# Storing the first five pairs of output batches two batches sooner in a batched matmul of two transposed operands

## The chip, the cores and the metric

The kernel runs on one core of a Trainium2 chip. The metric is the device time of one execution in microseconds (us), the median of several runs. The span that a profile shows is about 2 us shorter than the time measured for the same run. SyncE, ScalarE, VectorE and TensorE are called by these names; in the profile's lines they are SP, ACT, DVE and PE. A transfer between DRAM and SBUF, the core's working memory, is issued by SyncE or ScalarE, each of which has its own queue, and moved in packets by the core's 16 DMA engines. In the rows of 40 slices, DMA is the busy share of these engines in tenths (9 is 90% or more) and PEclk the clock granted to TensorE in tenths (9 is 90% or more, 5 is half).

## The reference

Sixteen independent products of 512 x 512 matrices, both operands transposed, in float32:

```python
def setup_inputs():
    batch, m, k, n = 16, 512, 512, 512
    return {"a": np.random.randn(batch, k, m).astype(np.float32),
            "b": np.random.randn(batch, n, k).astype(np.float32)}

def reference(a, b):
    return np.matmul(a.transpose(0, 2, 1), b.transpose(0, 2, 1)).astype(np.float32)
```

That is 33.55 MB to read and 16.78 MB to write.

## The kernel before

Batches go in eight pairs. SyncE's queue holds all loads, in program order, and at its end the stores of the last three pairs. ScalarE's queue holds the stores of pairs 0 to 4, between its casts and copies. VectorE casts and turns b (through TensorE's transposes); ScalarE casts a. There are three buffers for pairs of a, three for b, and five for pairs of output; the reuse of an output buffer is guarded by SyncE, which waits for an old store to land before it issues the load of a later pair's a.

```python
WIDE = range(1, 6)
LOADS = 3
PAIRS = 3
OUTS = 5
LAG = 3
TAIL = 3
H = B // 2
# ... cut ...
def run_sp(sp):
    for i in range(B):
        if i == 0:
            load_a(sp, 0)
        for p in ([0] if i == 0 else [(i + 1) // 2] if i % 2 and i + 1 < B else []):
            if p >= PAIRS:
                sp.wait_ge(turned, p - PAIRS + 1)
            sp.dma_start(b_sb[p % PAIRS][:], b_v[p]).then_inc(b_in[p % PAIRS], 16)
        if i % 2 == 0 and i // 2 >= OUTS:
            sp.wait_ge(o_out[i // 2 % OUTS], 16 * (i // 2 // OUTS))
        if i and not (i % 2 and i // 2 in WIDE):
            load_a(sp, i)
    for j in range(H - TAIL, H - 1):
        sp.wait_ge(summed, MO * (2 * j + 2) + 3)
        store(sp, j)
    # ... the last pair goes in two halves: cut ...

def run_act(act):
    cast_a(act, 0)
    for i in range(B - 1):
        cast_a(act, i + 1)
        copy_out(act, i, slice(2, 4), oa_go)
        j, odd = divmod(i - LAG, 2)
        if odd and 0 <= j < H - TAIL:
            store(act, j)
    # ... cut ...

# TensorE, per pair:
with pe.Fori(0, H) as _i:
    half(0, 0)
    half(0, 1)
    take(bt_go)
    turn(0)
    half(1, 0)
    turn(1)
    half(1, 1)
```

`cast_a(act, i)` waits for batch i's load; `half(x, h)` is half of a batch's sums, 8 matmuls. The loads of pairs 1 to 5 (WIDE) are one transfer of 2.1 MB in contiguous runs of 16 KB; batches 12 to 15 are loaded one by one, in runs of 8 KB, as stores are.

## Time and profile before

| | before |
|---|---|
| time, median | 124.49 us (124.38 to 124.84, 3 runs) |
| span of the profile | 122.5 us |
| bytes moved | 50.33 MB, of it 39.85 on SyncE's queue |
| TensorE, VectorE, ScalarE busy | 68%, 46%, 55% |
| a pair's loads at the full rate | 9.8 us |
| a pair's compute (stores of ScalarE at 43.55, 54.10, 64.66) | 10.5 us |

No engine is near its limit on the average; what is full is the transfers.

### The profile page before, as it was taken

Reading aid. Unit: us, or ns where it says so; the run is one execution under the profiler, and the core shown is the slowest. Engines: PE = TensorE matmul, PEld = TensorE weight load, DVE = VectorE, ACT = ScalarE, POOL = GpSimd, SP = SyncE. Lnnn points to the kernel's source line nnn. Section 1 sums busy time; section 2 is a strip of 40 time slices with the busy share of each in tenths; the row PEclk is TensorE's granted clock in tenths of the full one; section 3 lists DMA queues with packets and bytes.
Section 4 is the critical chain, followed back from the end, with each engine's and each line's share of the span. In section 5 each row is a group of like instructions: output and inputs, shape, how many; then the busy total and the mean of one; then the engine's idle time right before and its main releaser. Section 6 shows DMA issues by size and latency. Waiting matters only on the chain. (4 is left out here: it accounts for less than half of the span.)

```text
span 122.5 us, 1093 instructions
## 1 busy us (share of the span) xinstructions
PE 83.3 (68%) x400; PEld 48.0 (39%) x400; DVE 56.0 (46%) x48; ACT 66.9 (55%) x44; POOL 0.7 (1%) x6
## 2 busy tenths in 40 slices
PE   0000949799799979979994950593999599798000
PEld 0000913464365446437543610131744464374000
DVE  0005272837839575692759340039295542703000
ACT  4140015684997999799797008997221864803000
POOL 2000000000000000000000000000000000000000
PEclk9999999999999999999999997569999999999855
DMA  3999999999999999999999999999999999999992
GB/s 67 447 428 428 415 442 428 434 428 428 428 428 428 428 428 415 407 423 431 442 407 452 420 431 436 431 409 452 423 409 428 428 428 425 428 428 428 428 425 120
DMA packets 4928, 50.33 MB, mean 411 GB/s; under 512 B 448, under 2 KB 448, under 8 KB 448
## 3 DMA queue, kind: packets, MB, share of 16 engines
q1 hardware_dynamic: 3568, 39.85, 77.1%
q10 hardware_dynamic: 1360, 10.49, 20.2%
HBM read 33.55 MB, written 16.78 MB: 411 GB/s over the span
## 5 line engine op out<-in xcount | busy, mean ns | idle before, releaser
L256 PE MATMUL o_ps<-bt_sb,a_bf 128*128 128x512 bf16 x256 | 64.9, 402 | 8.7 <-PEq L231 8.2
L256 PEld LDWEIGHTS o_ps<-bt_sb,a_bf 128*128 128x128 bf16 x256 | 28.8, 116 | 38.7 <-issue 16.4
L164 ACT CAST a_bf<-a_sb 64x2048 bf16<-64x2048 f32 x20 | 38.0, 1899 | 7.6 <-DMA a_sb<-in_a_dram 7.3
L242 PE MATMUL bt_ps<-identity,b_bf 128*128 128x128 f32 x144 | 22.1, 302 | 20.8 <-PEq L231 20.8
L176 DVE COPY o_sb<-o_ps 128x1024 f32<-128x1024 f32 x16 | 19.6, 1224 | 29.9 <-PE o_ps L256 29.9
L242 PEld LDWEIGHTS bt_ps<-identity,b_bf 128*128 128x128 f32 x144 | 20.5, 209 | 25.7 <-issue 24.5
L189 DVE CAST b_bf<-b_sb 128x2048 bf16<-128x2048 f32 x16 | 19.4, 1219 | 22.7 <-DMA b_sb<-in_b_dram 22.7
L176 ACT COPY o_sb<-o_ps 128x1024 f32<-128x1024 f32 (+1 forms) x17 | 16.4, 964 | 19.7 <-PE o_ps L256 19.6
L166 ACT CAST a_bf<-a_sb 128x2048 bf16<-128x2048 f32 x6 | 11.4, 1901 | 18.4 <-DMA a_sb<-in_a_dram 18.4
L198 DVE COPY bt_sb<-bt_ps 128x1024 f32<-128x1024 f32 x16 | 19.4, 1214 | 2.7 <-PE bt_ps L242 2.7
L166 ACT ACT_TABLE_LOAD x1 | 1.3, 1283 | 0.9 <-PEq L302 0.9
L143 POOL TENSOR_SCALAR_AFFINE_SELECT identity<-identity 128x128 f32<-128x128 f32 x1 | 0.3, 292 | 0.2 <-POOL identity L141 0.2
L141 POOL MEMSET identity<- 128x128 f32 x1 | 0.2, 204 | 0.7 <-POOLq L54 0.7
L302 POOL MEMSET const-bfloat16-1.0<- 128x1 bf16 x1 | 0.1, 102 | 0.0
L302 POOL MEMSET const-uint8-127<- 128x1 uint8 x1 | 0.1, 102 | 0.0
L302 POOL MEMSET const-float32-0.0<- 128x1 f32 x1 | 0.1, 99 | 0.2 <-issue 0.2
L302 POOL MEMSET const-float32-1.0<- 128x1 f32 x1 | 0.1, 99 | 0.0
## 6 DMA issues: line engine op xcount, KB each, us to landing
b_sb<-in_b_dram SPq DMA_DIRECT2D x8, 2048.0 KB, 20.4
a_sb<-in_a_dram SPq DMA_DIRECT2D x5, 2048.0 KB, 19.0
out_dram<-o_sb ACTq DMA_DIRECT2D x5, 2048.0 KB, 16.2
a_sb<-in_a_dram SPq DMA_DIRECT2D x6, 1024.0 KB, 16.2
out_dram<-o_sb SPq DMA_DIRECT2D x2, 2048.0 KB, 13.3
out_dram<-o_sb SPq DMA_DIRECT2D x2, 1024.0 KB, 8.9
```

The costliest lines, as they stand in the source:

```text
L141: pool.memset(identity[:], 0.0).then_inc(id_go, 1)
L143: pool.affine_select(out=identity[:], in_=identity[:], compare_op=mybir.AluOpType.not_equal, fill=1.0, base=0, pattern=[[-1, P]], channel_ ...
L164: copy = act.copy(to[s * P // 2:(s + 1) * P // 2], x[own, s * KO:(s + 1) * KO, :])
L166: copy = act.copy(to[:], x[:, g * KO:(g + 1) * KO, :])
L176: copy(o_sb[i // 2 % OUTS][:, i % 2, rm, :], o_ps[h][:, p, :]).then_inc(go, 1)
L189: dve.tensor_copy(to, x).then_inc(bc_go, n)
L198: dve.tensor_copy(bt_sb[g][:].rearrange("p j (ni r) -> p j ni r", r=NR), bt_ps[:].rearrange("p j r (g ni) -> p g j ni r", g=2)[:, g],).the ...
L242: last = pe.transpose(bt_ps[:, j, r, :], w[:, r, j, :], identity[:])
L256: last = pe.matmul(o_ps[h][:, q, :], a_r[:, rk, 2 * h + q, :], bt_h[:, rk // 2, rk % 2, :], start=(rk == 0), stop=(rk == KO - 1),)
L302: nc = _bacc.Bacc("TRN2", target_bir_lowering=False, num_devices=1)
```

## The change

The intent: a pair is complete in SBUF when the batch behind it has been copied out, so it may be stored then. The output buffer comes free sooner, SyncE's waits for stores shrink, and the stores are spread over more of the run. Five stores on ScalarE's queue are each issued two batches sooner; nothing else moves.

```diff
-    LAG = 3
+    LAG = 1
```

## The prediction

> **What bounds the kernel now.** I read the page's slices first. The DMA row says 9 in every slice but the first and the last.
>
> ```profile
> span 122.5 us, 1093 instructions
> ...
> PE   0000949799799979979994950593999599798000
> ...
> DMA  3999999999999999999999999999999999999992
> GB/s 67 447 428 428 415 442 428 434 428 428 428 428 428 428 428 415 407 423 431 442 407 452 420 431 436 431 409 452 423 409 428 428 428 425 428 428 428 428 425 120
> ...
> q1 hardware_dynamic: 3568, 39.85, 77.1%
> q10 hardware_dynamic: 1360, 10.49, 20.2%
> ```
>
> The reader is to see that the transfers are never out of work, and that the rate is the same when only loads run (to slice 14, about 44 us) and when loads and stores mix. The 38 full slices (116.4 us) move 50.33 MB less the ends' 0.57: 0.4275 MB per us. The first slice's 67 GB/s puts the first byte at 2.6 us, the last slice's 120 the last byte at 120.3; the span ends 2.2 us later. So no order of the same bytes can win more than about 1%; an order can only lose, by leaving the transfers dry.
>
> Second, the waits of the queue that issues the loads, and the SyncE timeline after 82 us, for what the stores hold back:
>
> ```profile
> SPq L104 <- DMA out_dram<-o_sb: 17.2, 2, 11.9
> SPq L102 <- DMA out_dram<-o_sb: 15.8, 1, 15.8
> ```
>
> ```profile
> 94.12 0.40 SPq L89 DMA_DIRECT2D out_dram<-o_sb  x1
> 105.28 0.39 SPq L89 DMA_DIRECT2D out_dram<-o_sb  x1
> 109.17 0.34 SPq L89 DMA_DIRECT2D out_dram<-o_sb  x1
> 113.48 0.34 SPq L89 DMA_DIRECT2D out_dram<-o_sb  x1
> ```
>
> SyncE stands 33 us before the a-loads of pairs 5, 6 and 7, until the stores of pairs 0, 1 and 2 have landed, as output buffers are reused. The last store, of batch 15, is issued at 113.48, its 1.05 MB take 2.45 us, and the last byte moves at 120.3: so it waited behind a backlog until 117.85. The first load was issued at 0.89 and its byte moved at 2.6, a lead of 1.7 us; the last store could have started at 115.2. The compute at the end thus has 2.65 us of slack over the transfers.
>
> Third, ScalarE's timeline, for what sets that compute end:
>
> ```profile
> 43.55 0.42 ACTq L89 DMA_DIRECT2D out_dram<-o_sb  x1
> ...
> 95.33 1.90 ACT L166 CAST a_bf<-a_sb 128x2048 bf16<-128x2048 f32 x1 [3.17 <-DMA a_sb<-in_a_dram]
> ...
> 103.70 1.90 ACT L166 CAST a_bf<-a_sb 128x2048 bf16<-128x2048 f32 x1 [0.36 <-DMA a_sb<-in_a_dram]
> ```
>
> The cast at 95.33 is batch 13's: it waited for its load. From there to the last issue at 113.48 is 18.15 us of cast and work that is mostly TensorE without long gaps. The load of batch 13 therefore starts the tail.
>
> **What the Trainium skill says.** "DMA: Bandwidth & Descriptors", section "Issuing engines are not separate DMA queues": transfers from SyncE and ScalarE run on the same 16 engines. The trace agrees: 428 GB/s with one queue and with two. The same page, "Queues, rings and completion order": each engine goes round its rings packet by packet. The packet counts agree with one packet per contiguous run: q1 is 3200 packets of data and 23 transfers x 16 of completion. A b-load or a paired a-load is in runs of 16 KB; a single a-load (batches 12 to 15) and a store are in runs of 8 KB. So I take a ScalarE store to get 1/3 beside a wide load and 1/2 beside a single one. Does the trace hold with it? The store of pair 0 is issued at 43.55 and moves from 45.25. Loads alone have moved 18.24 MB by then; at 0.285 MB/us the end of pair 5's b (22 MiB of loads, 23.07 MB) is 62.2, plus 0.7 to be seen 62.9. The cast of it began at 62.50. In the end stage pair 6's b is seen at 81.5, so its bytes ended at 80.8; store 3 is issued at 83.49 and moves from 85.2. Until then loads alone move 1.88 MB (batch 12's and 0.83 of pair 7's b); the other 1.27 MB of that b at 0.285 ends at 89.7, and batch 13's 1.05 MB at half of 0.4275 ends at 94.6, seen at 95.3: the trace has 95.33. The rule stands for this kernel. "HBM Reference", "Bandwidth": a core alone gets well above the 358 GB/s share; the trace's 428 agrees.
>
> **The change part by part.** Nothing is added or removed: the order of instructions is the same on TensorE, VectorE, SyncE and GpSimd; ScalarE's list holds the same five stores, each two batches earlier. An issue is 0.38 us of ScalarE's sequencer, as before: no cost. No buffer is freed wrongly: store j goes when batch 2j+2 is summed, which cannot be before both copies of batch 2j+1.
>
> What moves is bytes. Store 0 goes when batch 2 is summed, at 33.0 (TensorE's batch ends there), not 43.55; it moves from 34.7. By then loads alone have moved 13.7 MB (13.1 MiB). Order of loads in MiB, cumulative: b3 14, a of pair 3 16, b4 18, a4 20, b5 22, a5 24, b6 26, batch 12 27, b7 29, batch 13 30, batch 14 31, batch 15 32. At 2/3 rate one pair's 4.19 MB takes 14.7 us, and one store's 2.1 MB at 1/3 takes 14.7 too: both rings stay full and go in step. Compute needs 10.5 us a pair (stores 43.55, 54.10, 64.66), so it begins to wait for loads at about 50 us.
>
> Seen times by the rule: b3 38.7 (its cast ran at 39.19), a3 46.1 (45.60), b4 53.4 (49.72), a4 60.8 (56.12), b5 68.2 (62.50), a5 75.6 (73.94), b6 83.0 (81.55). So the loads come later from 46 us on, but the long stop before pair 5 nearly evens it out. Stores 0, 1, 2 end at 49.4, 64.1, 78.8. They release SyncE at about 51.7, 66.4 and 81 (store landing is some 2.3 us after), when the load ring still has work until 67.5, 82 and 99: those 33 us of waiting shrink or stop mattering, and gain nothing, since the transfers did not starve then.
>
> Then batch 12 at half rate 4.9 us: 87.9; b7 7.4 us: 95.3; batch 13 4.9 us: 100.2. Store 3 ends at 91, store 4 (issued by about 84, when batch 10 is summed) at 102. Batch 14 is seen at 103.9, batch 15 at 106.4, the latest they can be: 33.55 MB of loads and all five stores, 44.04 MB.
>
> Batch 13 comes at 100.2 in place of 95.33, 4.9 us later, because 9.95 MB of stores went ahead of it, not about 7.9. b7 at 95.3 leaves the tail free at about 100.2 too: cast, copy-out and turn at 1.2 us each, then 0.3 and 1.0 of transposes; batch 13's cast ends 102.1, so batch 13 leads. With 18.15 us behind it the last store is issued at 118.35. Stores 5, 6 and half of 7 (5.24 MB) run from 105.7 to about 119, with a small gap before store 6, issued near 110. So the last store finds an empty ring: 118.35 + 1.7 + 2.45 + 2.2 = 124.7 of span, against 122.5. The slip of 4.9 less the slack of 2.65 is the same 2.2. The measured time is 2.0 above the span: 126.7. A new ring under load may take about a microsecond longer to start (store 0 of before landed 18.7 us after issue), which takes some 0.3 off: 126.5, or +1.6%.
>
> **The rivals.** First: nothing happens. If stores get less than their share, batch 13 comes at 98 or sooner, the slip is under 2.65 us and the backlog hides it: 124.4 to 124.8. For it: the store of pair 0 took 18.7 us, not 14.7 + 2.3. Against it: the end-stage landing is met to 0.1 us. Second: faster, as SyncE's 33 us of waits for stores go and the 7.3 and 9.9 us stalls of ScalarE and VectorE before pairs 5 and 6 with them. Against it: DMA is 9 in those slices; the stalls ran beside stores that had to move anyway. Even complete success would give less than 1.2 us (the clearer start and end): 123.3 to 124.5. Third: worse than the sum. If all five stores move before batch 13, it is seen at (31.46 + 10.49)/0.4275 + 2.6 + 0.7 = 101.4: 127.9. And more waits of TensorE can drop its clock: at 78 us, after 6.0 us idle, 16 matmuls took 5.41 us where 3.9 is usual. Two gaps of 2 to 3 us are foreseen in the tail; gaps of 2 us kept the clock, so this is a chance, of up to 1.5 us: 128 to 129.
>
> **Range and chances.** The centre is 126.5; the first rival sets the low end, 124.8, the third the high end, 128.1. The 2% line is at 127.0, half a microsecond above the centre, so slower has 0.38, within 2% 0.61, and faster 0.01, for want of any idle transfer to win.
>
> **What would show it.** Stores of ScalarE issued at about 33, 43.5, 54, 69 and 84. Casts waiting for b4 near 53 and pair 5's a near 75. SyncE's waits for stores much shorter. Batch 13's cast near 100 and the last store near 118; last DMA slices at less than 9, and a GB/s row that dips just before the end. It would be wrong if the slices stay 9 to 120 us (the backlog held), if batch 13 lands before 98, or if the middle shows an idle DMA slice, which would mean a load held back longer than I think.

## The result, and the profile after

Before: 124.66 us (124.38 to 124.90, 4 runs). After: 128.34 us (128.15 to 128.50, 4 runs). The ratio is 1.0295, with a 95% interval of 1.0265 to 1.0325. Ratios are the mean time of one kernel's fast runs over that of the other's in the same rounds, so not quite the ratio of the medians.

The page of the kernel after: span, granted TensorE clock, DMA share and rate in 40 slices of 3.16 us.

```profile
span 126.3 us, 1085 instructions
...
PEclk9999999999999999769999959999999855999996
DMA  3999999999999999999999999999999999909975
GB/s 75 454 431 446 394 441 441 431 426 446 400 337 431 449 418 431 431 426 439 439 413 441 415 423 436 420 426 436 433 436 415 423 428 431 423 31 374 415 332 208
```

The row of nines now has a hole: a slice of 0, at 31 GB/s, near 110 us, and two slices under 9 at the end. The windows view of the kernel after measures it (columns: stretch, its length, the busy time of each engine, the granted clock, the DMA share, GB/s):

```profile
110.00:111.00 1.00, 0.92 (x5) 0.43 (x5) 0.00 (x0) 0.79 (x1) 0.00 (x0) 1.00 0.70 295
111.00:114.00 3.00, 3.00 (x14) 1.30 (x12) 1.73 (x2) 2.03 (x2) 0.00 (x0) 1.00 0.00 0
114.00:121.00 7.00, 5.78 (x32) 3.79 (x32) 1.85 (x2) 1.85 (x3) 0.00 (x0) 1.00 1.01 419
121.00:122.00 1.00, 0.00 (x0) 0.00 (x0) 0.00 (x0) 0.33 (x1) 0.00 (x0) 1.00 0.51 213
```

The idle shares sum to 0.3 + 3.0 + 0.5 = 3.8 us, and the span grew from 122.5 to 126.3, by 3.8. So the whole loss is transfers that stood idle at the end; the middle shows no idle transfers. In the middle the DMA row is as full as before.

Why idle? SyncE's timeline of the kernel after, end part, has the stores that were left:

```profile
97.01 0.40 SPq L89 DMA_DIRECT2D out_dram<-o_sb  x1
...
113.17 0.39 SPq L89 DMA_DIRECT2D out_dram<-o_sb  x1
```

```profile
117.06 4.64 SPq L89 DMA_DIRECT2D out_dram<-o_sb  x2
```

The stores of pairs 5, 6 and 7 were issued at 94.12, 105.28, 109.17 and 113.48 before. Now pair 6's comes at 113.17, when by the packet records nothing has moved since 111.3 (its own first packet moves at 114.1), and the last one at 121.36 (117.06 + 4.64, less its own 0.34). Each waits for compute, and ScalarE's timeline of the kernel after shows what compute waited for:

```profile
31.43 0.42 ACTq L89 DMA_DIRECT2D out_dram<-o_sb  x1
...
101.99 1.90 ACT L166 CAST a_bf<-a_sb 128x2048 bf16<-128x2048 f32 x1 [6.94 <-DMA a_sb<-in_a_dram]
...
104.70 1.90 ACT L166 CAST a_bf<-a_sb 128x2048 bf16<-128x2048 f32 x1
```

The first store went out at 31.43, not 43.55. The cast of batch 13 waited 6.94 us for its load and began at 101.99; before it began at 95.33. That load came 6.66 us later because all five of ScalarE's stores had moved ahead of it: by the packet records of the trace the fifth store ended at 101.2 and batch 13's load at 101.1. (Before, the same loads, but only about 7.8 MB of the 10.49 MB of stores, had moved when batch 13's load ended, at 94.6.)

What the change was to improve, it improved: the waits of SyncE's queue for stores, after, are 12.0 us in place of 33.0.

```profile
SPq L104 <- DMA out_dram<-o_sb: 6.7, 2, 4.4
SPq L102 <- DMA out_dram<-o_sb: 5.3, 1, 5.3
```

That gained nothing, as these waits had not left the transfers idle.

The rest of the delay of the last store is on TensorE. Its timeline, before, from the start of batch 13's first eight matmuls:

```profile
97.53 1.98 PE L256 MATMUL o_ps<-bt_sb,a_bf 128*128 128x512 bf16 x8 [0.47 <-PEq L231]
```

and after, with the transposes ahead of them:

```profile
100.73 1.95 PE L242 MATMUL bt_ps<-identity,b_bf 128*128 128x128 f32 x8 [2.85 <-PEq L231]
104.19 3.23 PE L256 MATMUL o_ps<-bt_sb,a_bf 128*128 128x512 bf16 x8 [1.50 <-PEq L231]
```

The eight transposes took 1.95 us where 1.20 is usual, the eight matmuls 3.23 where 1.98 is usual; the 5 5 in the clock row says why. TensorE idled 2.85 us, as pair 7's b came late (its cast waited until 96.95), and its clock was halved. Only the slower matmuls delay the end: the transposes were done before batch 13's cast ended, at 103.89.

### The profile page after: what moved, and what is told of

It reads as the page before. It is cut to its first block, busy times and chain, and to the rows that moved or that the text cites. A ratio compares the mean times of both kernels' runs of the same rounds, so it can differ in the third digit from the quotient of the medians.

```text
span 126.3 us, 1085 instructions
## 1 busy us (share of the span) xinstructions
PE 84.5 (67%) x392; PEld 49.1 (39%) x400; DVE 56.1 (44%) x48; ACT 66.7 (53%) x44; POOL 0.7 (1%) x6
## 3 DMA queue, kind: packets, MB, share of 16 engines
q10 hardware_dynamic: 1360, 10.49, 19.6%
## 5 line engine op out<-in xcount | busy, mean ns | idle before, releaser
L256 PE MATMUL o_ps<-bt_sb,a_bf 128*128 128x512 bf16 x248 | 63.7, 405 | 9.3 <-PEq L231 8.5
L242 PE MATMUL bt_ps<-identity,b_bf 128*128 128x128 f32 x144 | 23.3, 313 | 26.9 <-PEq L231 26.9
L242 PEld LDWEIGHTS bt_ps<-identity,b_bf 128*128 128x128 f32 x144 | 21.4, 210 | 31.9 <-issue 30.8
```

What stands on the lines that cost most here:

```text
L242: last = pe.transpose(bt_ps[:, j, r, :], w[:, r, j, :], identity[:])
L256: last = pe.matmul(o_ps[h][:, q, :], a_r[:, rk, 2 * h + q, :], bt_h[:, rk // 2, rk % 2, :], start=(rk == 0), stop=(rk == KO - 1),)
```

## The experiments

There were eleven runs. In the expectations, theory A is the one that the prediction rests on: the last stores hide behind a backlog of transfers until the compute at the end slips too far, and it slips when stores move ahead of the last loads. Its rivals are that the two queues lose rate while they mix or that the many stalls in the middle cost the time (together theory B), and that only the last stores count. For each kernel the table has the start of the cast of batch 13 (in its profile), the issue of the last store, and the span of that profile.

| kernel | time, median | batch 13's cast | last store issued | span | span less issue |
|---|---|---|---|---|---|
| before | 124.49 | 95.33 | 113.48 | 122.46 | 8.98 |
| last two stores late | 124.58 | 95.56 | 113.68 | 122.5 | 8.8 |
| one batch sooner | 124.38 | 96.92 | 116.45 | 122.5 | 6.0 |
| fifth store behind the loads | 124.46 | 97.13 | 117.74 | 122.7 | 5.0 |
| filled gap | 126.16 | 100.66 | 118.64 | 123.5 | 4.9 |
| last two stores soon | 125.98 | 98.80 | 119.33 | 124.2 | 4.9 |
| filled gap, again | 126.30 | 101.80 | 119.76 | 124.7 | 4.9 |
| peeled only | 127.77 | 101.10 | 120.74 | 125.6 | 4.9 |
| change, again | 128.35 | 101.62 | 121.11 | 126.0 | 4.9 |
| change | 128.34 | 101.99 | 121.36 | 126.3 | 4.9 |
| swapped loads | 130.65 | 94.50 | 123.57 | 128.5 | 4.9 |

Read it from the right. From the fifth row on, the span ends 4.9 us after the last store's issue: no backlog delays it. Above that the span is 122.5 to 122.7, whatever the issue: the backlog hides it. The bend is where issue + 4.9 = 122.5, at 117.6, so compute had 117.6 - 113.5 = 4.1 us of slack over the transfers: that much later could the last store be issued at no cost. The two runs that the table leaves out, stores in runs of 4 KB and two batches later, lost time before the end.

### One batch sooner in place of two

```diff
-    LAG = 1
+    LAG = 2
```

> Every store one batch sooner than before, one later than in the change. Theory A (backlog at the end): the time stays at that of before unless the load of batch 13 comes more than about 2.65 us later than the 95.3 us of before. Stores start at about 42 us here, and the rule of 1/3 and 1/2 puts batch 13's cast near 97: 124.4 to 125.2 us. Theory B (the two queues lose rate while they run together, or TensorE's stalls cost by their number): the loss grows with the stretch in which both run, so about half of the 3.7 us: 126.0 to 126.8.

Measured: 124.38 us, ratio to before 1.0001 (0.9981 to 1.0020). SyncE's last issue in this run, and its DMA row:

```profile
116.45 0.34 SPq L89 DMA_DIRECT2D out_dram<-o_sb  x1
```

```profile
DMA  2999999999999999999999999999999999999993
```

The last store is 2.97 us later than before, and not a nine is missing. A dose of half the change costs none of the 3.7 us. Theory A's threshold is there; a cost that grows with the mixed stretch is not. TensorE's clock was halved here too (batch 13's first eight matmuls took 3.40 us), so that of the 2.97 us only 1.59 are the cast's delay; the slack hid both.

### The last two stores as late as before

```diff
-                j, odd = divmod(i - LAG, 2)
-                if odd and 0 <= j < H - TAIL:
-                    store(act, j)
+                for j in range(H - TAIL):
+                    if i == 2 * j + 1 + (LAG if j < 3 else 3):
+                        store(act, j)
```

> Stores of pairs 0 to 2 as soon as in the change, those of pairs 3 and 4 as late as before. Theory A: the middle looks like the change (casts wait for each pair's loads), but fewer stores go ahead of batch 13's load, whose cast begins at about 96: 124.3 to 125.0 us. Theory B (mixing, or the stalls of the middle, cost the time): the middle is that of the change, so most of its loss stays: 127 to 128.5.

Measured: 124.58 us, ratio 1.0024 (1.0003 to 1.0044). The middle of this run is like the change's: VectorE waits 3.40, 4.15 and 3.36 us for the b of pairs 4, 5 and 6, in the same places as in the change (5.71, 5.74, 4.48), where before it waited 2.17 us for pair 5's and 9.86 for pair 6's alone. Yet the loss is gone. So three early stores and stalls in the middle are harmless by themselves; the bytes that go ahead of the last loads count.

### The last two stores alone two batches sooner

```diff
+                for j in range(H - TAIL):
+                    if i == 2 * j + 1 + (3 if j < 3 else LAG):
+                        store(act, j)
```

(in place of the same three lines)

> Stores of pairs 0 to 2 as late as before, those of pairs 3 and 4 two batches sooner. Theory A: the store queue doesn't run empty between stores 2 and 3, batch 13's cast begins at about 98.4, a slip of 3.1 us, little over the 2.65 of slack: 124.5 to 125.8 us. Theory B: the middle is that of before until about 65 us, and only some 10 us more of mixing: 125.0 to 125.5. Another rival, that the last two stores alone make the loss: 127.5 to 128.5.

Measured: 125.98 us, ratio 1.0088 (1.0019 to 1.0157); three runs lie at 125.95 to 126.12 and one at 124.37. The median is just above theory A's range (124.5 to 125.8), and above theory B's. Batch 13's cast began at 98.80 (98.4 expected), a slip of 3.5 us, which is inside the slack of 4.1. But from that cast to the last issue it took 20.5 us, not 18.15: TensorE's clock was halved from 100 to 106 us, its eight matmuls took 3.57 us and the transposes behind them 1.91:

```profile
100.99 3.57 PE L256 MATMUL o_ps<-bt_sb,a_bf 128*128 128x512 bf16 x8 [2.12 <-PEq L231]
104.36 1.91 PE L242 MATMUL bt_ps<-identity,b_bf 128*128 128x128 f32 x8
```

These two are 2.4 us over their usual 1.98 and 1.11, which is the difference between 20.5 and 18.15. So the profiled run lost by the clock: with 18.15 us the last store would have been issued at 116.95, before the bend. It fits that the one run at 124.37 escaped the halving, but that run has no profile, so this is argued and not shown. The two stores alone make less than half of the loss.

### The fifth store behind all loads

```diff
-    TAIL = 3
+    TAIL = 4
```

With TAIL 4 SyncE issues pair 4's store too, after the last load, in the same ring.

> The change, but the store of pair 4 is issued by SyncE behind all loads in place of ScalarE: the same bytes, 2.1 MB fewer of them ahead of the last loads. Theory A: stores 0 to 3 end near 90 us, loads run alone after it, batch 13's cast begins at about 97.2, a slip of 1.9 us, under the slack: 124.4 to 125.3 us, DMA row full to the end. Theory B: middle and stalls as in the change: 127 to 128.5.

Measured: 124.46 us, ratio 1.0008 (0.9987 to 1.0029). One store of 2.1 MB moved out of the way of the last loads takes back all of the 3.7 us, though the other four go as early as in the change. Here batch 13's cast at 97.13 no longer waited for its load, but for ScalarE's copy-out of the batch before; the last store was issued at 117.74, at the bend, and the span is 122.7.

### A filled gap on TensorE, and its control

```diff
+            def fill(n):
+                for _ in range(n):
+                    pe.transpose(o_ps[0][:, 0, 0:P], identity[:], identity[:])
 ...
+            def pair(filled=False):
                 half(0, 0)
                 half(0, 1)
+                if filled:
+                    take(od_go)
+                    fill(8)
                 take(bt_go)
                 turn(0)
+                if filled:
+                    fill(10)
-                half(1, 0)
+                half(1, 0, filled)
                 turn(1)
                 half(1, 1)
-            with pe.Fori(0, H) as _i:
+            with pe.Fori(0, H - 2) as _i:
+                pair()
+            pair(True)
+            pair()
```

The transposes write into a bank whose sums start anew right after, so the result stays right. The control has `pair()` in place of `pair(True)`.

> The change, with 18 needless transposes of the identity in pair 6's turn alone, where TensorE waits for batch 13's load, to keep its clock up (results unchanged: the sums written after them start anew). If the halved clock between 100 and 107 us cost what its rows say (8 matmuls 3.23 us in place of 1.99), the last store is issued 18.2 us after batch 13's cast begins in place of 19.4, and the time falls by about 1.2 us: 126.9 to 127.4. If the clock costs nothing (the work behind waits for something else), 128.1 to 128.6.

> The control of the filled gap: TensorE's last two pairs stand outside the loop as there, but without the 18 transposes. If the filling alone made the gain (2.2 us of median), this is the change again: 127.9 to 128.6. If taking the pairs out of the loop made it, or a part, it lies at 126 to 127.5.

> The filled gap once more, beside the change and the control: 125.4 to 126.8 if the first result holds, and 17.9 to 18.3 us from the start of batch 13's cast to the issue of the last store.

> The change itself, once more, on the chip of the control. Theory A says it repeats: 128.1 to 128.6, batch 13's cast within 1 us of 102, the clock halved for some us around 100 to 107, and 3 to 4.5 us of idle transfers between 110 us and the end. If the dip of the GB/s row at 35 us is a part of the mixing and not of one run, slices 10 and 11 again show under 410.

Measured: filled 126.16 (125.43 to 126.72) and 126.30 us (125.86 to 126.55); control 127.77 (127.27 to 128.35); the change again 128.35 (127.89 to 129.59). TensorE's timeline of the second filled run:

```profile
98.99 1.07 PE L248 MATMUL o_ps<-identity 128*128 128x128 f32 x8 [0.48 <-PEq L231]
100.28 1.20 PE L242 MATMUL bt_ps<-identity,b_bf 128*128 128x128 f32 x8 [0.22 <-PEq L231]
101.31 1.25 PE L248 MATMUL o_ps<-identity 128*128 128x128 f32 x10
104.07 1.75 PE L261 MATMUL o_ps<-bt_sb,a_bf 128*128 128x512 bf16 x7 [1.50 <-PEq L231]
```

Batch 13's matmuls run at the full clock again (1.75 us for the 7 that the trace holds). The same part of the repeat of the change, on the same chip:

```profile
100.20 1.20 PE L242 MATMUL bt_ps<-identity,b_bf 128*128 128x128 f32 x8 [1.43 <-PEq L231]
103.81 2.91 PE L256 MATMUL o_ps<-bt_sb,a_bf 128*128 128x512 bf16 x8 [2.42 <-PEq L231]
106.51 1.78 PE L242 MATMUL bt_ps<-identity,b_bf 128*128 128x128 f32 x8
```

From the cast to the last issue it is 17.96 us (101.80 to 119.76), against 19.49 in the repeat of the change (101.62 to 121.11), though both casts came at the same time. So the halved clock cost about 1.5 us here. (The filled kernel also takes VectorE's copy-out earlier than the control does, but pair 7's transposes start no sooner for it: 100.28 against 100.20.) The first expectation, a gain of 1.2, was too small: the median fell 2.0 to 2.2. Against the control, which has the same code outside the loop, it is 1.5 to 1.6. The control fell between its two expectations: half a microsecond lies between it and the change, and their runs overlap; whether it belongs to taking the pairs out of the loop is left open. Useless work on the idle engine was worth 1.2%, but did not bring back the time of before: the load comes late all the same.

The repeat shows what of one profile is chance. Batch 13's cast came at 101.62, the idle transfers are there (slices 34 to 38 of its GB/s row: 426 55 374 416 333), and slice 11 is again low, 338 where the first profile has 337 (slice 10 is not: 463 where the first has 400). The halving came at another place, as the lines above show: after gaps of 1.43 and 2.42 us.

### Batch 13's load ahead of pair 7's b

```diff
+                if i == 13:
+                    load_a(sp, i)
                 for p in (...):          # pair 7's b
 ...
-                if i and not (i % 2 and i // 2 in WIDE):
+                if i and i != 13 and not (i % 2 and i // 2 in WIDE):
```

> The change, with the load of batch 13 issued ahead of pair 7's b in place of behind it: the same bytes ahead of the later of the two. Theory A (the tail starts at the load that comes last ahead of batch 13's sums): batch 13 is seen near 94.5, pair 7's b near 102, and behind b lie two more copies and a turn, so batch 13's sums start 2.5 to 3.5 us later than in the change: 130.5 to 132 us. If batch 13's load isn't what the end hangs on: 128.1 to 128.6.

Measured: 130.65 us, ratio 1.0542 (1.0482 to 1.0601). VectorE's timeline of this run shows the cast of pair 7's b, and TensorE's the sums of batch 13:

```profile
101.28 1.23 DVE L191 CAST b_bf<-b_sb 128x2048 bf16<-128x2048 f32 x1 [8.10 <-DMA b_sb<-in_b_dram]
```

```profile
105.07 1.95 PE L244 MATMUL bt_ps<-identity,b_bf 128*128 128x128 f32 x8 [7.64 <-PEq L233]
106.81 2.80 PE L258 MATMUL o_ps<-bt_sb,a_bf 128*128 128x512 bf16 x8
```

Batch 13 was cast at 94.50, b at 101.28, and the sums began 2.6 us later than in the change (106.81 against 104.19): the bytes ahead are the same, but b has three more steps of VectorE to go before the sums. The end does hang on the load that comes last ahead of batch 13's sums.

### Stores in runs of 4 KB

```diff
-            eng.dma_start(
-                out_v[2 * j + part.start:2 * j + part.stop].rearrange(...),
-                o_sb[j % OUTS][:, part],
-            ).then_inc(...)
+            for m in ([slice(0, 2), slice(2, 4)] if j < H - TAIL else [slice(0, 4)]):
+                eng.dma_start(
+                    out_v[2 * j + part.start:2 * j + part.stop, :, m].rearrange(...),
+                    o_sb[j % OUTS][:, part, m],
+                ).then_inc(...)
```

(with the counts that are waited for made to fit)

> The change, with ScalarE's stores written in runs of 4 KB (two transfers a store, half the rows of each partition each) at the same times. If the share goes by packets, a store now gets 1/5 beside a 16 KB load in place of 1/3: store 0 takes some 25 us in place of 14.5, fewer store bytes go ahead of the loads, batch 13's cast begins before 98.5 and the time is 124.4 to 125.8. If the share goes by queue whatever the packets, nothing changes: 128 to 129, with batch 13's cast near 102.

Measured: 126.41 us, ratio 1.0176 (1.0141 to 1.0211). The time missed both expectations (124.4 to 125.8, and 128 to 129); what was said of the share and of the cast held. By the packet records store 0 took 23.0 us (35.7 to 58.7) in place of 14.7 (35.2 to 49.9): its share fell from a third to about a fifth, as packets in turn would have it. Batch 13's cast came at 96.37, and the last store was issued at 116.95, before the bend at 117.6. So the tail is healed; but the time is not that of before. The DMA row is full to the end, and what is lost is rate. The windows view of this run, in a stretch where mostly stores of 4 KB moved, shows one of the low places:

```profile
76.50:82.00 5.50, 3.36 (x16) 2.15 (x15) 4.62 (x4) 3.80 (x3) 0.00 (x0) 0.87 1.05 363
```

363 GB/s with the DMA engines busy; before, where stores of 8 KB moved alone (62.5 to 65.5 us), it was 421. The length of the runs alone does not explain it: the first two microseconds of this stretch, stores of 4 KB alone too, have 418 and 410 GB/s, the next two 320 and 381. Why the rate falls there is left open. That a store now takes longer also brought the waits of SyncE for stores back to 38.2 us, and with them this stretch of stores alone.

### Two batches later than before

```diff
-    LAG = 1
+    LAG = 5
```

> Every store two batches later than before. Theory A: loads run alone until store 0 is issued at about 54 us; the loads of pair 5's b end near 57, and pair 5's a waits for store 0 to land, so that the transfers have only stores, one at a time, and run dry for some us in the middle; the end is later by those: 126 to 130 us, with DMA slices below 9 between 55 and 75 us. Theory B (mixing costs): less mixing, so no slower than before: 124 to 124.6.

Measured: 133.28 us, ratio 1.0718 (1.0700 to 1.0736), more than expected. The page's rows:

```profile
DMA  3999999999999999996899994999977999999994
GB/s 92 466 399 439 417 437 459 404 434 444 399 444 434 414 454 409 434 407 277 234 379 451 404 412 80 359 437 432 384 274 269 372 424 439 417 434 424 429 427 182
```

The loads run out of buffers, wait for a store to land (48.7 us in all), and the transfers starve three times: near 60, 80 and 98 us. The least mixing makes the slowest kernel; that mixing as such costs the time is ruled out. Only the first of these holes was foreseen.

No version beats the kernel before. The best ones equal it, with transfers as full as its own.

## Why the prediction was right or wrong

**Transfers are the bound and no order can win.** Right for every order that was tried: none of the eleven runs is faster than before, and SyncE's waits for stores fell from 33.0 to 12.0 us for nothing.

**Issue times and the loads of the middle.** Right in kind, with luck at the start: store 0 was issued at 31.43 and not 33.0, and moved 3.8 us after its issue and not 1.7, so that its first packet, at 35.19, came close to the 34.7 that was said. Stores went at 31.4, 42.0, 56.8, 70.1 and 85.1 us (33, 43.5, 54, 69, 84 said). The casts of the b of pairs 4, 5 and 6 came at 54.55, 69.48 and 84.42, each 1.2 to 1.4 us after the time given.

**Batch 13's load leads the end.** Right; the swapped loads show it. Its size was wrong: 101.99 and not 100.2, a slip of 6.66 us and not 4.9. The term that failed is "9.95 MB of stores went ahead of it": it was 10.49, all five, which is the third rival's bound. 0.9 us of the error is there when pair 3's b is seen (39.62 against 38.7), beside a dip of the rate to 337 GB/s as the second queue starts, which both profiles of the change have (338 in the repeat). The rest is the share of 1/3, which came out at 34.4% of the full rate between 35.2 and 77.9 us (6.29 MB of stores at 0.147 MB per us). That the rule of shares had met the trace of before so closely was luck in part: it let stores 0 and 3 start 1.7 us after their issue, at 45.25 and 85.2, and their first packets moved at 47.37 and 87.12.

**18.15 us from that cast to the last issue.** Wrong. It took 19.37, as TensorE's clock was halved; 17.96 with the gap filled. The prediction had this as a chance of up to 1.5 us and left it out of the centre, as gaps of 2 us had kept the clock. Here a gap of 2.85 us did not.

**The slack of 2.65 us, and 6.35 us from the last issue to the end.** Both wrong by the same 1.45: they are 4.1 and 4.9. The start of a transfer in an empty queue was taken as 1.7 us, worked out from the rate in the first slice; the first packet of the run comes 1.0 us after its issue. The landing was oversized too: in the kernel after the last packet ends at 124.9 and the span at 126.3, 1.4 us and not 2.2.

**The sum.** Predicted for the span: 4.9 - 2.65 = 2.2 us. Measured: 6.66 + 1.22 - 4.08 = 3.80. The errors in the slip (1.8 and 1.2) stood against that in the slack (1.45), and 0.2 had been taken off for the slow start of a queue (126.7 to 126.5; the prediction calls it 0.3), so that the centre was 1.8 us short, and the time 0.2 above the stated range. The mechanism held. What failed is the size of two terms on the way to the last issue, the bytes ahead of batch 13's load and the 18.15 us behind it; an error in the slack hid half of that. The bytes were those of the third rival, the edge of the range: the fifth store ended at 101.20 in the change and 101.28 in its repeat, batch 13's load at 101.06 and 100.94.

## What to carry to other kernels

Where transfers are full from start to end and stay so, a new order of the queue gained nothing here, and what it left for the end decided what it cost (two batches later shows that the middle can also be made to run dry): keep enough stores back to cover the last compute, and let the last loads pass. Measure the slack (here the last store could be issued 4.1 us later at no cost), and compare with it the whole delay of that issue, that of the last needed load and what the engines add behind it; below the slack a change was free, above it each microsecond counted in full. A load that comes late can cost again, through the clock of TensorE, which idles for it (1.2 us in the profile of the change, 1.5 in its repeat).

## What the Trainium skill lacked or had wrong

- "DMA: Bandwidth & Descriptors", section "Latency and other measured facts", gives about 600 ns to the first byte for transfers issued by SyncE and ScalarE. Here the first packet of the first load came 1.0 us after the start of its issue (0.89 to 1.90), or 0.6 us after the issue's end at 1.27, which would agree; the page does not say from where it counts. That of a store whose queue joined a busy one came 3.8 us after the start of its issue (31.43 to 35.19; before, 43.55 to 47.37). No page has the loaded figure.
- The same page, "Where 436 GB/s comes from", says that the HBM side (about 358 GB/s) binds between HBM and SBUF. Loads, and loads mixed with stores, ran at 428 GB/s on this one core and stores alone at 421, so that limit did not bind here.
- A rate of stores on trn2 by the length of their runs was found on no page. Here stores alone ran at 421 GB/s in runs of 8 KB (62.5 to 65.5 us of before) and between 320 and 418 in runs of 4 KB (four single microseconds from 76.5); one stretch each, so no rule.
- "TensorE: Matmul & The Clock Gate", section "HAM oscillation — how this bites in real kernels", warns of idle gaps over about 3.4 us. In a gap of 2.85 us the clock was halved (97.88 to 100.73 us, the clock at 0.53 from 100 to 101), and in the repeat after two gaps of 1.43 and 2.42 us, while a gap of 3.20 us at 85 us of the first profile left it full, and one of 3.19 us in the repeat (84.48 to 87.67) did not. A threshold on the gap does not fit this; the free-running window of the same page, section "What's actually happening", allows for it.
